# A 32-byte copy on eight rows ahead of the first store of a streaming batch norm

## The chip, the cores and the metric

The kernel runs on one core of a Trainium2 chip. The metric is the time on the device in microseconds (us) of one execution; lower is better. The core has five engines that run side by side: TensorE (not used here), VectorE (DVE in the profile), ScalarE (ACT), GpSimd (POOL) and SyncE (SP). Data moves between the memory of the chip (DRAM) and the working memory of the core (SBUF, 128 partitions) through 16 DMA engines. A DMA is issued by SyncE, ScalarE or GpSimd; each issuer has a queue of its own on every one of the 16 DMA engines (q1 for SyncE, q10 for ScalarE, q0 for GpSimd in the profile), and a semaphore that counts to 16 says that all engines have finished their share.

## The reference

Batch normalisation with given mean and variance over an array x of 32 x 256 x 128 x 128 numbers in float32 (536.87 MB), with one factor and one offset for each of the 256 channels:

```python
eps = 1e-5
mean = running_mean.reshape(1, -1, 1, 1)
var = running_var.reshape(1, -1, 1, 1)
gamma = gamma.reshape(1, -1, 1, 1)
beta = beta.reshape(1, -1, 1, 1)
return gamma * (x - mean) / np.sqrt(var + eps) + beta
```

Everything is read once and written once, so 1073.7 MB cross the DMA engines.

## The kernel before

The array is cut into 64 tiles of 128 channels by 16384 numbers: 8.39 MB each, 64 KB in each of 128 partitions, one tile for each image and half of the channels. Three buffers in SBUF (NBUF = 3) hold tiles in turn; tile i lies in buffer i mod 3. An unused tile named pad, 936 numbers wide, lies ahead of them.

At the start SyncE issues the left half of tile 0, the four parameter vectors, the right half of tile 0, and tiles 1 and 2 (lines 89 to 98). VectorE turns the parameters so that a channel lies in each partition (par), and with one square root on ScalarE makes scale_t and shift_t for each channel. Then every tile is multiplied by its scale and increased by its shift in place.

ScalarE does this for whole tiles, one instruction each (line 142). Two tiles are shared: of tile 0 VectorE does the first 6784 columns (VHEAD) and ScalarE the other 9600; of the last tile VectorE does the first 9216 (VLAST) (line 131).

When ScalarE is through with a tile, the semaphore adone goes up by one, and the tile is stored. The stores of the first 61 tiles are issued by GpSimd, the last three by ScalarE (NTAIL = 3), all on line 173. The store of tile 0 also waits for VectorE's part through vdone. When a store from buffer s has landed, which the semaphore stored[s] counts, SyncE issues the load of the tile that comes into this buffer next (line 161). So the order is a ring: load, ScalarE, store, next load, with three tiles in it at any time. No scheduler decides the order; each engine's list of instructions is as it is written, and the DMA queues are served in the order of issue.

At the end GpSimd waits for its stores and drains, and SyncE waits for all stores (lines 177 to 185).

Of the kernel before, what the change touches and what calls it, by code (L numbers as in the profile page):

```python
# [9 lines left out]
PAD = 936  # L10
NHEAD = 3
NTAIL = 3
VHEAD = 6784
VLAST = 9216


@with_exitstack
def kernel(
    ctx: ExitStack,
    tc: tile.TileContext,  # L20
    x: bass.AP,
    gamma: bass.AP,
    beta: bass.AP,
    running_mean: bass.AP,
    running_var: bass.AP,
    out: bass.AP,
):
    nc = tc.nc
    eps = 1e-5
    f32 = mybir.dt.float32  # L30

    N, C, H, W = x.shape
    P = nc.NUM_PARTITIONS
    assert C % P == 0
    NCB = C // P
    HW = H * W
    NT = N * NCB
    B = 32
    NQ = P // B
    NE = 16  # L40
    NPAR = 4

    xr = x.rearrange("n (cb p) h w -> (n cb) p (h w)", p=P)
    outr = out.rearrange("n (cb p) h w -> (n cb) p (h w)", p=P)

    params = ctx.enter_context(tc.tile_pool(name="params", bufs=1))
    data = ctx.enter_context(tc.tile_pool(name="data", bufs=1))
    params.tile([P, PAD], f32, name="pad", tag="pad")
    bufs = [data.tile([P, HW], f32, name=f"t{s}", tag=f"t{s}") for s in range(NBUF)]
    rows = params.tile([B, NPAR * C], f32, name="rows", tag="rows")  # L50
    turned = params.tile([B, NPAR * C], f32, name="turned", tag="turned")
    par = params.tile([P, NPAR, NCB], f32, name="par", tag="par")
    eps_t = params.tile([P, 1], f32, name="eps_t", tag="eps")
    std_t = params.tile([P, NCB], f32, name="std_t", tag="std")
    rstd_t = params.tile([P, NCB], f32, name="rstd_t", tag="rstd")
    scale_t = params.tile([P, NCB], f32, name="scale_t", tag="scale")
    ms_t = params.tile([P, NCB], f32, name="ms_t", tag="ms")
    shift_t = params.tile([P, NCB], f32, name="shift_t", tag="shift")

    loaded = [tc.alloc_semaphore(f"loaded{s}") for s in range(NBUF)]
    stored = [tc.alloc_semaphore(f"stored{s}") for s in range(NBUF)]
    closed = [tc.alloc_semaphore(f"closed{s}") for s in range(NBUF)]
    early = tc.alloc_semaphore("early")
    first = [tc.alloc_semaphore(f"first{s}") for s in range(NHEAD)]
    vdone = tc.alloc_semaphore("vdone")
    adone = tc.alloc_semaphore("adone")
    fetched = tc.alloc_semaphore("fetched")
    vec = tc.alloc_semaphore("vec")  # L70
    act = tc.alloc_semaphore("act")

    with tc.tile_critical():  # L73
        count = [0]

        def step(inst, sem=None, value=None):
            if sem is not None:
                inst._wait_ge(sem, value)
            elif count[0]:
                inst._wait_ge(vec, count[0])  # L80
            inst.then_inc(vec, 1)
            count[0] += 1
            return count[0]

        left, right = slice(0, HW // 2), slice(HW // 2, HW)
        last = NT - 1


        nc.sync.dma_start(out=bufs[0][:, left], in_=xr[0][:, left]).then_inc(early, 16)
        zeroed = step(nc.vector.memset(rows[:], 0.0))  # L90
        for r, ap in enumerate((running_var, gamma, beta, running_mean)):
            inst = nc.sync.dma_start(out=rows[0:NE, r * C : (r + 1) * C], in_=ap.partition_broadcast(NE))  # L92
            if r == 0:
                inst._wait_ge(vec, zeroed)
            inst.then_inc(fetched, 16)
        nc.sync.dma_start(out=bufs[0][:, right], in_=xr[0][:, right]).then_inc(first[0], 16)  # L96
        for i in range(1, NHEAD):
            nc.sync.dma_start(out=bufs[i][:], in_=xr[i]).then_inc(first[i], 16)

        def landed(i):  # L100
            if i < NHEAD:
                return first[i], 16
            s = i % NBUF
            before = 1 if s < NHEAD else 0
            return loaded[s], 16 * (i // NBUF + 1 - before)


        step(nc.vector.memset(eps_t[:], eps))  # L108
        step(nc.vector.transpose(out=turned[:], in_=rows[:]), fetched, 16 * NPAR)  # L109
        blocks = turned.rearrange("p (rc q b) -> p rc q b", q=NQ, b=B)  # L110
        flat = par.rearrange("p r cb -> p (r cb)")
        for q in range(NQ):
            placed = step(nc.vector.tensor_copy(out=flat[q * B : (q + 1) * B], in_=blocks[:, :, q, 0]))  # L113
        var_t, gamma_t, beta_t, mean_t = (par[:, r] for r in range(NPAR))
        nc.scalar.activation(  # L115
            out=std_t[:],
            in_=var_t,
            func=mybir.ActivationFunctionType.Sqrt,
            bias=eps_t[:],
            scale=1.0,  # L120
        )._wait_ge(vec, placed).then_inc(act, 1)
        step(nc.vector.reciprocal(out=rstd_t[:], in_=std_t[:]), act, 1)  # L122
        step(nc.vector.tensor_mul(out=scale_t[:], in0=gamma_t, in1=rstd_t[:]))  # L123
        step(nc.vector.tensor_mul(out=ms_t[:], in0=mean_t, in1=scale_t[:]))  # L124
        ready = step(nc.vector.tensor_sub(out=shift_t[:], in0=beta_t, in1=ms_t[:]))  # L125
        nc.vector.wait_ge(vec, ready)
        nc.scalar.wait_ge(vec, ready)

        def vector_part(i, first_col, end):
            t, cb = bufs[i % NBUF], i % NCB  # L130
            return nc.vector.tensor_scalar(  # L131
                out=t[:, first_col:end],
                in0=t[:, first_col:end],
                scalar1=scale_t[:, cb : cb + 1],
                scalar2=shift_t[:, cb : cb + 1],
                op0=mybir.AluOpType.mult,
                op1=mybir.AluOpType.add,
            ).then_inc(vdone, 1)

        def scalar_part(i, first_col):  # L140
            t, cb = bufs[i % NBUF], i % NCB
            return nc.scalar.activation(  # L142
                out=t[:, first_col:],
                in_=t[:, first_col:],
                func=mybir.ActivationFunctionType.Identity,
                bias=shift_t[:, cb : cb + 1],
                scale=scale_t[:, cb : cb + 1],
            ).then_inc(adone, 1)


        def share(i):
            return VHEAD if i == 0 else VLAST if i == last else 0

        vector_part(0, 0, VHEAD)._wait_ge(early, 16)
        nc.scalar.wait_ge(early, 16)
        vector_part(last, 0, VLAST)._wait_ge(*landed(last))


        for i in range(NHEAD, NT):
            s = i % NBUF  # L160
            inst = nc.sync.dma_start(out=bufs[s][:], in_=xr[i])
            if i >= NBUF:
                inst._wait_ge(stored[s], 16 * (i // NBUF))
            inst.then_inc(loaded[s], 16)

        for i in range(NT):
            eng = nc.gpsimd if i < NT - NTAIL else nc.scalar
            packet = {"single_packet": True} if i < NT - NTAIL else {}
            written = (stored if i < NT - NTAIL else closed)[i % NBUF]
            scalar_part(i, share(i))._wait_ge(*landed(i))  # L170
            if i in (0, last):
                eng.wait_ge(vdone, 1 if i == 0 else 2)
            eng.dma_start(out=outr[i], in_=bufs[i % NBUF][:], **packet)._wait_ge(adone, i + 1).then_inc(  # L173
                written, 16
            )


        for s in range(NBUF):
            nc.gpsimd.wait_ge(stored[s], 16 * ((NT - NTAIL - s + NBUF - 1) // NBUF))
        nc.gpsimd.drain()  # L180

        for s in range(NBUF):
            nc.sync.wait_ge(stored[s], 16 * ((NT - NTAIL - s + NBUF - 1) // NBUF))
            nc.sync.wait_ge(closed[s], 16)
# [30 lines left out]
```

## Time and profile before

| what | value |
|---|---|
| median of 3 runs | 2501.97 us (2497.04 to 2505.49) |
| the profiled execution's own time | 2502.17 us |
| its span, first to last instruction | 2500.4 us |
| ScalarE busy | 886.8 us |
| VectorE busy | 12.4 us |
| GpSimd busy | 32.7 us |
| moved by the DMA engines | 1073.84 MB, 429 GB/s over the span |
| a whole tile on ScalarE | 14.04 us |
| a load, issue to landing, median | 53.5 us |
| a store from GpSimd, issue to landing, median | 48.8 us |

The profile is of one execution, so sums are made against its own 2502.17 us, 0.20 us over the median; 1.8 us of it lie outside the span. Busy times of the engines are shares of the span. "DMA" rows give the mean busy share of the 16 DMA engines in tenths, one digit for each of 40 equal slices, and "GB/s" what they moved in each. The trace also holds a record of every DMA packet with its queue, start, length and size; a number said to be from the packet records is counted there. A row of the chain of waits has its start in us, its length in us, and what it was; a row of the timeline has the same, then the instruction, and in brackets how long the engine had been idle and what ended that.

### The profile page before, as it was taken

How to read it: one execution, taken by the hardware profiler on the slowest of the kernel's cores; microseconds unless marked ns; L12 is line 12 of the kernel's file. 1: busy time of each engine (PE TensorE's matmuls, PEld its weight loads, DVE VectorE, ACT ScalarE, POOL GpSimd, SP SyncE). 2: the span in 40 equal slices, each digit the busy share in tenths (PEclk: the TensorE clock that was granted, in tenths of full speed). 3: DMA queues.
4: the chain of work that ended last, by engine and by line, in shares of the span. 5: the costliest groups of instructions: out<-in, count | busy, mean ns of one | idle time of the engine just before them, and what ended most of it. 6: DMA issues, size and time to landing. Idle time of an engine off the chain costs nothing.

```text
span 2500.4 us, 276 instructions
## 1 busy us (share of the span) xinstructions
DVE 12.4 (0%) x13; ACT 886.8 (35%) x66; POOL 32.7 (1%) x65
## 2 busy tenths in 40 slices
DVE  1000000000000000000000000000000000000000
ACT  3243342433424234243342433424334243342422
POOL 0000000000000000000000000000000000000000
DMA  9999999999999999999999999999999999999997
GB/s 420 436 428 429 432 436 436 435 434 436 435 428 429 433 435 436 435 436 433 434 426 432 435 434 436 425 433 436 434 436 432 423 423 433 423 433 431 428 435 336
DMA packets 18707, 1073.84 MB, mean 429 GB/s; under 512 B 2128, under 2 KB 2192, under 8 KB 2192
## 3 DMA queue, kind: packets, MB, share of 16 engines
q1 hardware_dynamic: 9488, 536.94, 49.8%
q0 software_dynamic: 8784, 511.71, 47.5%
q10 hardware_dynamic: 432, 25.17, 2.3%
q14 instruction: 3, 0.02, 0.0%
HBM read 536.94 MB, written 536.87 MB: 429 GB/s over the span
## 4 chain that ended last, share of the span: by engine, by line
another core or an unknown queue 62%; ACT 35%; DMA 2%; issue 0%; SPq 0%; DVE 0%; ACTq 0%; DVEq 0%
ACT t L142 35%; DMA t<-in_x_dram 2%; SPq L92 0%; DVE rows L90 0%; ACTq L173 0%; SPq L96 0%; DVE eps_t L108 0%; DVEq L210 0%; SPq L73 0%
## 5 line engine op out<-in xcount | busy, mean ns | idle before, releaser
L142 ACT ACTIVATE t<-t,shift_t,scale_t 128x16384 f32<-128x16384 f32 (+1 forms) x64 | 885.2, 13831 | 1574.1 <-DMA t<-in_x_dram 1574.1
L173 POOL DMA_DIRECT2D out_dram<-t x61 | 32.5, 534 | 2332.7 <-ACT t L142 2332.7
L131 DVE TENSOR_SCALAR t<-t,scale_t,shift_t 128x6784 f32<-128x6784 f32 (+1 forms) x2 | 8.9, 4446 | 2448.3 <-DMA t<-in_x_dram 2448.2
L115 ACT ACTIVATE std_t<-par,eps_t 128x2 f32<-128x2 f32 x1 | 0.3, 295 | 14.3 <-DVE par L113 14.3
L115 ACT ACT_TABLE_LOAD x1 | 1.3, 1283 | 0.9 <-SPq L73 0.9
L109 DVE STREAM_TRANSPOSE turned<-rows 32x1024 f32<-32x1024 f32 x1 | 1.2, 1233 | 12.2 <-DMA rows<-in_running_mean_dram 12.2
L90 DVE MEMSET rows<- 32x1024 f32 x1 | 0.9, 912 | 1.2 <-SPq L73 1.2
L113 DVE COPY par<-turned 32x8 f32<-32x8 f32 x4 | 0.6, 162 | 0.1
L122 DVE RECIPROCAL rstd_t<-std_t 128x2 f32<-128x2 f32 x1 | 0.2, 165 | 0.4 <-ACT std_t L115 0.4
L124 DVE TENSOR_TENSOR ms_t<-par,scale_t 128x2 f32<-128x2 f32 x1 | 0.2, 161 | 0.0
L125 DVE TENSOR_TENSOR shift_t<-par,ms_t 128x2 f32<-128x2 f32 x1 | 0.2, 161 | 0.0
L123 DVE TENSOR_TENSOR scale_t<-par,rstd_t 128x2 f32<-128x2 f32 x1 | 0.2, 160 | 0.0
L199 POOL MEMSET const-bfloat16-1.0<- 128x1 bf16 x1 | 0.1, 102 | 0.0
L199 POOL MEMSET const-float32-0.0<- 128x1 f32 x1 | 0.1, 98 | 0.2 <-issue 0.2
L199 POOL MEMSET const-float32-1.0<- 128x1 f32 x1 | 0.1, 98 | 0.0
L199 POOL MEMSET const-uint8-127<- 128x1 uint8 x1 | 0.1, 98 | 0.0
L108 DVE MEMSET eps_t<- 128x1 f32 x1 | 0.1, 59 | 0.1
## 6 DMA issues: line engine op xcount, KB each, us to landing
t<-in_x_dram SPq DMA_DIRECT2D x2, 4096.0 KB, 16.1
t<-in_x_dram SPq DMA_DIRECT2D x63, 53.5
out_dram<-t POOLq DMA_DIRECT2D x61, 48.8
out_dram<-t ACTq DMA_DIRECT2D x3, 31.8
rows<-in_running_var_dram SPq DMA_DIRECT2D x1, 16.0 KB, 11.3
rows<-in_gamma_dram SPq DMA_DIRECT2D x1, 16.0 KB, 11.1
rows<-in_beta_dram SPq DMA_DIRECT2D x1, 16.0 KB, 10.9
rows<-in_running_mean_dram SPq DMA_DIRECT2D x1, 16.0 KB, 10.9
```

The costliest lines, as they stand in the source:

```text
L90: zeroed = step(nc.vector.memset(rows[:], 0.0))
L109: step(nc.vector.transpose(out=turned[:], in_=rows[:]), fetched, 16 * NPAR)
L113: placed = step(nc.vector.tensor_copy(out=flat[q * B : (q + 1) * B], in_=blocks[:, :, q, 0]))
L115: nc.scalar.activation(out=std_t[:], in_=var_t, func=mybir.ActivationFunctionType.Sqrt, bias=eps_t[:], scale=1.0,)._wait_ge(vec, placed).t ...
L122: step(nc.vector.reciprocal(out=rstd_t[:], in_=std_t[:]), act, 1)
L123: step(nc.vector.tensor_mul(out=scale_t[:], in0=gamma_t, in1=rstd_t[:]))
L124: step(nc.vector.tensor_mul(out=ms_t[:], in0=mean_t, in1=scale_t[:]))
L125: ready = step(nc.vector.tensor_sub(out=shift_t[:], in0=beta_t, in1=ms_t[:]))
L131: return nc.vector.tensor_scalar(out=t[:, first_col:end], in0=t[:, first_col:end], scalar1=scale_t[:, cb : cb + 1], scalar2=shift_t[:, cb ...
L142: return nc.scalar.activation(out=t[:, first_col:], in_=t[:, first_col:], func=mybir.ActivationFunctionType.Identity, bias=shift_t[:, cb : ...
L173: eng.dma_start(out=outr[i], in_=bufs[i % NBUF][:], **packet)._wait_ge(adone, i + 1).then_inc(written, 16)
L199: nc = _bacc.Bacc("TRN2", target_bir_lowering=False, num_devices=1)
```

## The change

GpSimd issues one more DMA, before its first store: it copies eight rows of 8 numbers (32 bytes each) from the finished parameters par to the unused tile pad, both in SBUF. The copy waits for ScalarE's part of tile 0, as the first store does, and its completion adds 16 to a new semaphore, aside. Nothing reads the copy. GpSimd waits for aside before its drain at the end, and SyncE waits for it before its last waits for the stores. Nothing else is changed.

```diff
+HALF = 8
...
-    params.tile([P, PAD], f32, name="pad", tag="pad")
+    pad = params.tile([P, PAD], f32, name="pad", tag="pad")
...
+    aside = tc.alloc_semaphore("aside")
...
             if i in (0, last):
                 eng.wait_ge(vdone, 1 if i == 0 else 2)
+            if i == 0:
+                eng.dma_start(out=pad[0:HALF, 0 : NPAR * NCB], in_=flat[0:HALF])._wait_ge(adone, 1).then_inc(aside, 16)
             eng.dma_start(out=outr[i], in_=bufs[i % NBUF][:], **packet)._wait_ge(adone, i + 1).then_inc(
                 written, 16
             )
...
+        nc.gpsimd.wait_ge(aside, 16)
         nc.gpsimd.drain()
 
+        nc.sync.wait_ge(aside, 16)
         for s in range(NBUF):
             nc.sync.wait_ge(stored[s], 16 * ((NT - NTAIL - s + NBUF - 1) // NBUF))
```

`flat` is par with its four parameters and two channel halves as 8 numbers in a row.

## The prediction

> **What bounds the kernel now.** I read the busy shares first, then the DMA queues, then the chain of waits, then short windows of the DMA traffic, and last the packet records of the trace (start, length and size of each DMA packet).
>
> The page's busy lines and DMA lines:
>
> ```profile
> DVE 12.4 (0%) x13; ACT 886.8 (35%) x66; POOL 32.7 (1%) x65
> ...
> DMA  9999999999999999999999999999999999999997
> GB/s 420 436 428 429 432 436 436 435 434 436 435 428 429 433 435 436 435 436 433 434 426 432 435 434 436 425 433 436 434 436 432 423 423 433 423 433 431 428 435 336
> ...
> q1 hardware_dynamic: 9488, 536.94, 49.8%
> q0 software_dynamic: 8784, 511.71, 47.5%
> ```
>
> No compute engine is busy more than 35% of the span; the 16 DMA engines are busy everywhere but in the last slice. Loads (q1, from SyncE) and stores (q0, from GpSimd) share them evenly.
>
> The chain of waits repeats one piece of ACT and one wait for a landing, once per tile; five of its ACT pieces:
>
> ```profile
> 89.18 14.04 ACT t L142
> ...
> 205.25 14.04 ACT t L142
> ...
> 1493.84 14.04 ACT t L142
> ...
> 1919.94 14.04 ACT t L142
> ...
> 2389.77 14.05 ACT t L142
> ```
>
> The distance between pieces is the period of a tile. Between these five lie 3, 33, 11 and 12 periods: 38.69, 39.05, 38.74 and 39.15 us, 38.99 on the mean. A period moves one load and one store, 16.78 MB; per engine that is 16 packets of 65,536 bytes. The packet records give 2.418 us for nearly every such packet, whatever the queue, and starts 2.414 us apart: 16 of them are 38.63 us. So the first stretch runs at the pace of a DMA engine, and later ones lose up to 0.5 us a period.
>
> Where that loss sits is seen in two windows of the DMA view, the first of 36 us in slices of 0.9 us, the second of 40 us in slices of 1 us, each packet counted where it starts:
>
> ```profile
> GB/s 73 0 1165 0 510 655 0 1019 146 0 1165 0 291 874 0 947 218 0 1165 0 218 947 0 801 364 0 1165 0 73 1092 0 655 510 0 1165 0 73 1092 0 583
> ...
> GB/s 66 918 66 983 66 328 721 0 983 66 524 524 0 983 66 852 197 197 786 66 983 66 524 459 66 983 66 590 393 66 983 66 983 66 262 721 66 983 66 590
> ```
>
> In the first (38 to 74 us), 1165 GB/s in 0.9 us is 16 packets: all engines start together, and queues change after each packet. In the second (1000 to 1040 us) lone 66s are single packets: an engine has fallen out of step. The landings of each transfer, counted per engine, tell the rest: until 205 us all 16 arrive within 0.7 us; then three engines fall behind the other thirteen, by 2.5 us at 284 us, 12 at 1000 us and 21 from 1500 us on. The lagging ones have no idle time from their first packet at 2.0 us to their last at 2498.25 us. Their 1024 packets at 2.414 us are 2472.3 us; the other 24 us are stretched packets, above all the first packet of a load (2.5 to 3.7 us instead of 2.418). The kernel's end is these three engines' work, and the 24 us are all that can be won.
>
> **The change, part by part.**
>
> *The copy's issue on GpSimd.* It stands after the wait for VectorE's part and itself waits for ScalarE's, so it goes where the first store goes now, and the store behind it. The timeline's rows of this place:
>
> ```profile
> 23.51 8.39 ACT L142 ACTIVATE t<-t,shift_t,scale_t 128x9600 f32<-128x9600 f32 x1 [6.74 <-DMA t<-in_x_dram]
> 32.21 0.67 POOL L173 DMA_DIRECT2D out_dram<-t  x1 [31.76 <-ACT t L142]
> ...
> 50.48 14.04 ACT L142 ACTIVATE t<-t,shift_t,scale_t 128x16384 f32<-128x16384 f32 x1 [18.59 <-DMA t<-in_x_dram]
> 64.83 0.53 POOL L173 DMA_DIRECT2D out_dram<-t  x1 [31.96 <-ACT t L142]
> 74.63 0.33 SPq L161 DMA_DIRECT2D t<-in_x_dram  x1
> ```
>
> An issue takes 0.53 to 0.67 us, so the first store is issued 0.5 to 0.7 us later. The engines have two loads queued until about 60 us, so the delay is covered: a load packet goes where a store packet would have gone. Without that cover it would cost 0.7 us, or a whole turn of 2.4 us where a slot is missed; I take 0. In the packet records the first store packet starts at 37.49 us, 5.3 us after its issue.
>
> The Trainium skill, DMA: Bandwidth & Descriptors, section "Anatomy of one DMA — SWDGE (gpsimd) path", charges a GpSimd DMA about 2.0 us whatever its size. By that rule, with nothing beside it, the sum would be 2504; the trace's engines are busy through that time, so I keep 0, and 2 us would be inside the same verdict.
>
> *The copy's packets.* 8 packets of 32 bytes and 16 completion packets of 4 bytes. The records hold 4-byte packets of 9 ns and 1,024-byte packets of 46 ns: at most 0.06 us on an engine, 0.1 as the upper end.
>
> *The turns.* The queues alternate packet by packet, and a 4-byte packet is seen to take a turn of its own queue. So the copy costs the store one turn (completion) on eight engines and two (row and completion) on the eight that carry rows. A store turn lost is a load turn won: the store ends one turn (2.41 us) later and the loads end one earlier. Now a load lands 14.5 us, six turns, after the store before it (SyncE issues on the store's landing at 74.63, the load before lands at 89.16). After the change that is four turns (9.7 us) on one half and two (4.8 us) on the other, and the halves are a turn apart: one reads while the other writes. The next load, issued at the store's landing, needs about 1.0 us to its first packet (0.96 to 1.98 us at the start), so it comes in time even with two turns, by 3.8 us. Were a third turn lost, the load queue would be empty for a moment and the engine would serve stores. A store waits in front of its queue longer than now. No engine stands idle: 0 us.
>
> *The end.* The lost turns stay lost to the last tile, since no slot is free in between. At the end the lagging engines have four packets of the last but one store left when the last load lands at 2469.27 us, 9.66 us; the last store's first packet can come 2477.0, 7.7 us after. With loads ahead of stores more is left, so that cover grows. ±1 us.
>
> *The two added waits* (GpSimd before its drain, SyncE before its last waits) are for a copy that is over before 50 us. Behind them stand only waits for the last stores. 0 to 0.1 us.
>
> *The stretched packets.* This is the one open term, 24 us now. Nothing in the trace of before shows two halves a turn apart. Lower end: all periods at the 38.63 us of the packet lengths alone, 60 x (38.99 - 38.63) = 22 us less. Upper end: periods as in the worst short stretch, 205.25 to 284.34 us, 39.55 us: 60 x 0.56 = 34 us more. I take no difference: the three engines lost the same 0.4 us a period while their distance to the others grew through every relation of reading and writing, from 2 to 21 us, so the relation between engines does not set the loss; which engine it is does.
>
> Sum: 2502.17 (this execution; span 2500.4, 1.8 around it) + 0 + 0.1 + 0 = 2502.3; the execution is 0.2 over the median of the runs, so 2502.
>
> **The rivals.**
>
> *The stretching shrinks: faster.* With halves out of step, the three engines may not be caught in the bad spot at the first packet of a load, since that would come some 5 to 12 us after the load's issue, where it now comes 16.4 us after it (74.63 to 90.99 in the packet records). For it: between 1493.84 and 1919.94 us the period is 38.74, so the loss can nearly vanish for eleven tiles. Against it: that was with the three behind as well. Price: all periods at 38.74, 60 x 0.25 = 15 us, 2487; half of it 2494.
>
> *The stretching spreads: slower.* Now eight engines, not three, come last at each load's landing, and the stretched packets sit on those that come last. Where the three were in step with each other (1919.94 to 2389.77 us, 39.15 us) their first load packets took 2.6 to 3.7 us at the same time. With eight in step from the start the whole run could go like that or worse: 60 x 0.16 = 10 us, 2512; at twice that excess 2522. It decides from a mean period of 39.12 us on.
>
> *The copy takes no turns* (its packets come while the load packet before is still running, 34.55 to 37.5 us): then all stays in step and the time is that of before, within the forecast.
>
> *The lag is a property of the engines.* The Trainium skill, DMA: Bandwidth & Descriptors, section "Latency and other measured facts", says that DMA engines 7 and 15 are usually slower in traces and guesses at contention on the ports of GpSimd's descriptor rings. The trace agrees that a few fixed engines lag (three, by 21 us), and by that rule a copy at the start changes nothing.
>
> **How the numbers follow.** Forecast, no difference beyond 0.3% (7.5 us, about what a measurement of this kernel can tell from no change; the runs of before span 8.5 us), with the copy that takes no turns in it: 0.40. Stretching shrinks by more than a third of its 24 us: 0.29. Stretching spreads: 0.31, a little more, since its price has no ceiling while the gain is bounded by 24 us. The range runs from 2484 (nearly all won) to 2518 (a third to a half of the upper end). The time of the likeliest case alone would be 2495 to 2509.
>
> **What would show it.** Right: the copy's row and the first store 0.5 to 0.7 us apart on GpSimd; a window of 38 to 74 us in which no slice holds 16 packet starts but two groups of eight alternate; the first load of SyncE's loop issued 2.4 to 5 us later than 74.63, the third tile landed 2 to 5 us before 89.16; mean period 38.9 to 39.1 us. Wrong: the mean period below 38.87 (faster) or above 39.12 (slower), engines idle in the middle of the run, or a tail in which the last store waits.

## The result, and the profile after

The changed kernel takes 2487.78 us in the median of 22 runs (2485.61 to 2500.54); the kernel before, in 22 runs beside them, 2500.7 us (2483.61 to 2514.36). The ratio is 0.9959, 95% interval 0.9944 to 0.9975: faster by 0.4%. The profiled execution took 2490.27 us with a span of 2488.5 us, 11.9 us less than the one of before.

Busy time, DMA and issue lines of the page of the changed kernel:

```profile
span 2488.5 us, 278 instructions
...
DVE 12.4 (0%) x13; ACT 886.8 (36%) x66; POOL 33.4 (1%) x66
...
GB/s 420 423 438 437 436 423 436 438 438 423 436 438 437 429 432 436 437 434 428 436 436 436 429 431 438 433 429 436 437 436 429 434 437 437 430 432 437 436 431 358
...
t<-in_x_dram SPq DMA_DIRECT2D x63, 44.0
out_dram<-t POOLq DMA_DIRECT2D x61, 58.0
...
pad<-par POOLq DMA_DIRECT2D x1, 0.2 KB, 8.2
```

The engines do what they did before. New is the last group: a load now lands 44.0 us after its issue (53.5 before), a store 58.0 us after its issue (48.8 before). The sum of the two is about the same, 102.0 against 102.3 us. The copy lands 8.2 us after its issue.

The timeline around the first store of the changed kernel (start, length, instruction, idle time before it):

```profile
23.38 8.39 ACT L144 ACTIVATE t<-t,shift_t,scale_t 128x9600 f32<-128x9600 f32 x1 [6.87 <-DMA t<-in_x_dram]
32.07 0.66 POOL L176 DMA_DIRECT2D pad<-par  x1 [31.62 <-ACT t L144]
32.72 0.57 POOL L177 DMA_DIRECT2D out_dram<-t  x1
45.76 14.04 ACT L144 ACTIVATE t<-t,shift_t,scale_t 128x16384 f32<-128x16384 f32 x1 [13.99 <-DMA t<-in_x_dram]
...
79.59 39.03 SPq L163 DMA_DIRECT2D t<-in_x_dram  x2
84.48 14.04 ACT L144 ACTIVATE t<-t,shift_t,scale_t 128x16384 f32<-128x16384 f32 x1 [24.68 <-DMA t<-in_x_dram]
```

The store is issued 0.65 us after the copy. Tile 1 is there at 45.7 us (50.5 before), tile 2 at 84.45 us (89.16 before), and SyncE issues its first load of the loop, on the landing of the first store, at 79.59 us (74.63 before). So the stores moved back by 5.0 us and the loads forward by 4.7 us: two turns of 2.41 us each. The next load now lies issued for 4.9 us before the load ahead of it has landed, not for 14.5 us.

The DMA traffic from 38 to 74 us, in slices of 0.9 us, shows that this holds for all 16 engines:

```profile
GB/s 0 874 291 0 291 874 0 874 291 0 1165 0 73 1092 0 874 291 0 1165 0 0 1165 0 728 437 0 1165 0 0 1165 0 510 655 0 1019 146 0 1165 0 364
```

1165 GB/s is again 16 packets that start in one slice. There are no two groups of eight. The packet records say why: at 36.8 to 37.3 us eight engines have a 32-byte packet of the copy, and at 37.1 to 37.5 us the other eight have a 4-byte packet instead; at 39.2 to 40.0 us all 16 have a 4-byte completion. Every engine has lost two store turns.

Where the time went, by the landings of the loads: tile 2 lands 4.7 us earlier; the 58 periods from there to tile 60 take 38.81 us on the mean in place of 38.995, 10.7 us in all; from the landing of tile 60 to the last store it is 151.2 us in place of 147.8, 3.4 us more. 4.7 + 10.7 - 3.4 = 12.0 us. What the shift gives at the start is mostly paid back at the end; the gain is in the periods. In the changed kernel one engine lags instead of three. In the landings of the stores it comes 12 us behind its nearest neighbour from about 1500 us on, and almost all of that is lost before 1330 us. In the landings of the loads the 16 engines stay within 4.4 us of each other up to tile 61, where the kernel before had 21 us between the first and the last. The windows view, before and then after, from 1900 to 2400 us (stretch, length, busy times, clock, DMA share, GB/s):

```profile
1900.00:2400.00 500.00, 0.00 (x0) 178.70 (x13) 6.37 (x12) 1.00 1.00 429
```

```profile
1900.00:2400.00 500.00, 0.00 (x0) 182.51 (x13) 6.40 (x12) 1.00 1.00 434
```

The DMA engines are busy all the time in both; in the changed kernel they move 434 GB/s, which is what they moved from 74 to 230 us in either.

### The profile page after: what moved, and what is told of

It is laid out like the page before. It is cut to its first block, busy times and chain, and to the rows that moved or that the text cites. A ratio compares the mean times of both kernels' runs of the same rounds, so it can differ in the third digit from the quotient of the medians.

```text
span 2488.5 us, 278 instructions
## 1 busy us (share of the span) xinstructions
DVE 12.4 (0%) x13; ACT 886.8 (36%) x66; POOL 33.4 (1%) x66
## 4 chain that ended last, share of the span: by engine, by line
another core or an unknown queue 93%; DMA 4%; SPq 1%; ACT 1%; issue 0%; DVE 0%; POOL 0%; DVEq 0%
DMA t<-in_x_dram 2%; DMA out_dram<-t 2%; SPq L163 1%; ACT t L144 1%; SPq L94 0%; DVE rows L92 0%; POOL pad L176 0%; DVE eps_t L110 0%; DVEq L216 0%; SPq L75 0%
## 5 line engine op out<-in xcount | busy, mean ns | idle before, releaser
L111 DVE STREAM_TRANSPOSE turned<-rows 32x1024 f32<-32x1024 f32 x1 | 1.2, 1232 | 11.9 <-DMA rows<-in_running_mean_dram 11.9
## 6 DMA issues: line engine op xcount, KB each, us to landing
rows<-in_running_mean_dram SPq DMA_DIRECT2D x1, 16.0 KB, 10.7
```

## The experiments

Three theories stood at first. Theory 1: what helps is the shift by two turns. Theory 2: the copy itself helps, by moving the descriptor ring on or by warming GpSimd's way of issuing a DMA. The third, the split into halves, was the forecast's and is tried on its own below. "Turns" is the distance from a store's landing to the next load's landing, in turns of 2.41 us; "lying time" is how long a load lies issued until the load ahead of it has landed on the last engine; the median of the load's issue-to-landing time less one period (38.7 us) gives it within 0.4 us. "Stretch" is the time by which the first packets of loads exceed 2.418 us in one execution, summed over the engines, counting packets over 2.44 us.

| kernel | turns | lying time, us | mean period from tile 2 to 60, us | stretch, us | median, us | ratio to before, 95% |
|---|---|---|---|---|---|---|
| before | 6 | 14.5 | 38.995 | 49 | 2500.7 | 1 |
| after | 2 | 5.1 | 38.81 | 6 | 2487.78 | 0.9959 (0.9944 to 0.9975) |
| e_early | 6 | 14.5 | 39.00 | 37 | 2506.77 | 1.0025 (1.0005 to 1.0045) |
| e_late2 | 2 | 5.1 | 38.725 | 12 | 2490.05 | 0.9971 (0.994 to 1.0003) |
| e_undo | 6 | 14.5 | 39.07 | 67 | 2506.08 | 1.0018 (0.9998 to 1.0038) |
| e_phi10 | 7 to 8 | 19.3 | 38.96 | 92 | 2510.93 | 1.0027 (0.9996 to 1.0058) |
| e_late1 | 4 | 9.7 | 39.125 | 49 | 2511.67 | 1.0029 (1.0008 to 1.0049) |
| e_delay | 8 | 6.1 | 38.81 | 11 | 2491.56 | 0.995 (0.993 to 0.997) |
| e_half | 6 and 2 | 13.4 | 38.76 | 40 | 2491.04 | 0.9966 (0.9933 to 0.9998) |
| e_mid | 6, then 2 | 14.5, then 5.1 | 38.79 | 33 | 2500.66 | 0.9984 (0.9956 to 1.0011) |
| e_delay8 | 6 | 5.7 | 38.76 | 12 | 2489.78 | 0.9945 (0.9923 to 0.9966) |
| e_delay4 | 6 | 10.1 | 39.06 | 31 | 2507.28 | 0.9991 (0.9969 to 1.0013) |
| e_late1_delay4 | 4 | 5.2 | 38.93 | 22 | 2495.33 | 0.9946 (0.9925 to 0.9967) |
| e_late2_delay2 | 4 | 7.4 | 38.96 | 31 | 2501.43 | 0.9974 (0.9949 to 1.0) |

Times and ratios are of 9 to 22 runs; the four columns before them are of one profiled execution each, so a row's period need not stand for its median. Single runs scatter: of the 22 of the kernel before, three lie below 2488 us, and of the 22 of the changed kernel two lie above 2500 us. None of these five was profiled. The kernels of the first four experiments (to e_phi10), of the next four and of the last four were run together; the kernel before had medians of 2503.5, 2504.9 and 2504.6 us beside them, and each ratio is to the runs beside it.

### The copy without the lost turns: e_early

```diff
+        nc.gpsimd.dma_start(out=pad[0:HALF, 0 : NPAR * NCB], in_=flat[0:HALF])._wait_ge(vec, placed).then_inc(aside, 16)
         var_t, gamma_t, beta_t, mean_t = (par[:, r] for r in range(NPAR))
...
-            if i == 0:
-                eng.dma_start(out=pad[0:HALF, 0 : NPAR * NCB], in_=flat[0:HALF])._wait_ge(adone, 1).then_inc(aside, 16)
```

> The copy is issued at about 16 us, as soon as the parameters are in place, long before the first store; its packets then take no turn from a store. Theory 1 (turns: what helps is that the store stream starts two turns later, so that a load lands 2 turns after a store and not 6): the distance from a store's landing to the next load's landing is again 14.5 us, and the time is that of the kernel before, ratio 0.998 to 1.002. Theory 2 (the copy itself: the descriptor ring moved on, or GpSimd's DMA path warmed): ratio 0.994 to 0.998 as in the changed kernel.

The copy's and the loads' issue lines:

```profile
t<-in_x_dram SPq DMA_DIRECT2D x63, 53.5
...
pad<-par POOLq DMA_DIRECT2D x1, 0.2 KB, 6.9
```

The copy is there, the loads land after 53.5 us as before the change, and the gain is gone: 1.0025 (1.0005 to 1.0045). That speaks against theory 2.

### The lost turns without the copy: e_late2

```diff
-VHEAD = 6784
+VHEAD = 1152
```

> No copy. VectorE has 1152 columns of tile 0 in place of 6784, so ScalarE's part takes about 4.8 us longer and the first store is issued at about 37.0 us in place of 32.2, two turns later. Theory 1: distance store landing to load landing 4.8 us (2 turns), SyncE's first loop load issued at about 79.5 us, ratio 0.994 to 0.998. Theory 2: no copy, so ratio 1.000 to 1.003.

```profile
t<-in_x_dram SPq DMA_DIRECT2D x63, 43.8
out_dram<-t POOLq DMA_DIRECT2D x61, 57.9
```

SyncE's first loop load is issued at 79.25 us, and the issue lines above are those of the changed kernel. The median is 2490.05 us, the ratio 0.9971 with an interval that just reaches 1.0003: eight of the twelve runs lie between 2484 and 2495 us, four between 2500 and 2519. Theory 1 has the better of it, but the two-turn state alone does not make every run fast.

### Taking the turns back: e_undo and e_phi10

Both add one DMA on SyncE, the first to the changed kernel, the second to the kernel before (with pad named as in the change). At the end SyncE waits for it, too:

```diff
+            if i == 2:
+                nc.sync.dma_start(out=pad[0:16, 16:24], in_=gamma[0:8].partition_broadcast(16)).then_inc(slot, 16)
             nc.sync.dma_start(out=bufs[i][:], in_=xr[i]).then_inc(first[i], 16)
```

> The changed kernel, and SyncE puts a DMA of 16 rows of 32 bytes between the loads of tiles 1 and 2, whose row and completion packets take two turns from the loads on each engine. Theory 1: the distance goes back to 6 turns (14.5 us) with the copy still in place, ratio 0.998 to 1.002. Theory 2: ratio 0.994 to 0.998.

> The kernel before, with only that DMA of 16 rows between the loads of tiles 1 and 2: the loads lose two turns. Theory 1: distance 10 turns (24 us); if the loss grows with the distance, ratio 1.002 to 1.008. Theory 2: ratio 0.999 to 1.001.

The issue line of the loads in e_undo:

```profile
t<-in_x_dram SPq DMA_DIRECT2D x63, 53.5
```

With the copy in place but the loads two turns back, the kernel is as slow as before, 1.0018 (0.9998 to 1.0038): theory 1 again. In e_phi10 the first loads came out at 10 turns as meant (24.2 us), but the store queue then ran empty and the distance settled between 17 and 19.5 us; the loads lie issued for 19.3 us, the stretch of their first packets is the largest of all, 92 us, and the median 2510.93 us. The interval does not exclude 1.

### Is it the distance, or how early the load is issued? e_late1 and e_delay

If only the distance counted, four turns should lie between six and two.

```diff
-VHEAD = 6784
+VHEAD = 3968
```

> No copy; VectorE has 3968 columns of tile 0 in place of 6784, so the first store is issued about 2.4 us later, one turn. Distance from a store's landing to the next load's landing 9.7 us (4 turns). If the loss grows with this distance: between the 6-turn and the 2-turn kernels, ratio 0.996 to 1.000; if only two turns help, 0.999 to 1.002.

It does not. The issue line of the loads:

```profile
t<-in_x_dram SPq DMA_DIRECT2D x63, 48.8
```

The loads lie issued for 9.7 us, and the kernel is slower than the one before, 1.0029 (1.0008 to 1.0049). The loss does not fall evenly with the distance.

The second kernel leaves the first store alone and holds back the loads. VectorE, which is idle in the loop, writes zeros to pad NPAUSE times after each store's landing, and SyncE waits for that; VectorE's part of the last tile comes after the loop.

```diff
+NPAUSE = 12
...
-                inst._wait_ge(stored[s], 16 * (i // NBUF))
+                nc.vector.wait_ge(stored[s], 16 * (i // NBUF))
+                for k in range(NPAUSE):
+                    paused += 1
+                    nc.vector.memset(pad[:], 0.0).then_inc(later, 1)
+                    nc.vector.wait_ge(later, paused)
+                inst._wait_ge(later, paused)
```

> The kernel before, with the first store where it was, but SyncE's loop loads wait for 12 small memsets that VectorE does after the store has landed, about 10 us. The distance on the slowest engine stays 14.5 us (6 turns); only the load is issued later, some 4.5 us before the slowest engine needs it, so the other engines cannot read ahead of it by more than that. Theory 1a (what counts is beside which store packet a load begins, so the distance): time as before, ratio 0.999 to 1.002, first packets of loads stretched as before (37 to 67 us in sum over the engines). Theory 1b (what counts is how long a load lies issued before the slowest engine begins it, so how far the others run ahead): ratio 0.994 to 0.998, with the stretch of first packets near the 6 to 12 us of the 2-turn kernels.

The lines of the loop and of its issues:

```profile
L168 DVE MEMSET pad<- 128x936 f32 x732 | 613.4, 838 | 1781.0 <-DMA out_dram<-t 1605.2 <-DVE pad L168 175.8
```

```profile
t<-in_x_dram SPq DMA_DIRECT2D x63, 44.7
out_dram<-t POOLq DMA_DIRECT2D x61, 43.6
```

A memset took 0.84 us and the wait between two 0.26 us, so the pause was 13.2 us and not the 10 that were meant. The load queue ran dry once a period and the distance went to 19.4 us, 8 turns. Yet all twelve runs lie between 2488 and 2496 us, ratio 0.995 (0.993 to 0.997), and the stretch is 11 us. A larger distance with a short lying time is fast, which points to the lying time. The other half of what was expected failed: the other engines still ran up to 17 us ahead of the last one before the last two loads, so it is not that they are held close.

### Doses of the pause: e_delay8, e_delay4, e_late1_delay4, e_late2_delay2

The same kernel with NPAUSE 8 and 4; and with NPAUSE 4 and VHEAD 3968, NPAUSE 2 and VHEAD 1152.

> 8 memsets in place of 12, so SyncE's loop loads are issued 8.8 us after the store's landing and lie issued 5.7 us before the slowest engine needs them; the load queue does not run empty and the distance stays 14.5 us (6 turns). If the time a load lies issued is what sets the loss: ratio 0.993 to 0.997, mean period of tiles 11 to 60 38.6 to 38.75. If the 12 memsets helped because the load queue ran empty (distance 19.4 us in that run): ratio 0.999 to 1.002.

> 4 memsets: loads issued 4.4 us after the landing, lying issued about 10 us, as in the 4-turn kernel; distance 14.5 us. If the lying time sets the loss with a limit between 5.7 and 9.7 us: ratio 0.999 to 1.003. If any pause on VectorE helps: 0.994 to 0.998.

> The 4-turn kernel (3968 columns on VectorE, no copy), which lost 0.3%, with 4 memsets: loads lie issued 5.3 us in place of 9.7. If the lying time sets the loss: ratio 0.993 to 0.997. If the distance of 4 turns is bad for itself: 1.001 to 1.005.

> The 2-turn kernel without a copy (1152 columns on VectorE) with 2 memsets: loads lie issued about 2.7 us in place of 4.9, still in time for the slowest engine. If a shorter lying time helps further: ratio 0.992 to 0.996, without the runs above 2500 us that the 2-turn kernel had. If 5 us is already enough: 0.994 to 0.998, the same as at 2 turns.

The timeline of e_delay8 around its first loop load:

```profile
75.61 0.84 DVE L168 MEMSET pad<- 128x936 f32 x1 [54.18 <-DMA out_dram<-t]
...
83.31 0.84 DVE L168 MEMSET pad<- 128x936 f32 x1 [0.26 <-DVE pad L168]
84.18 40.47 SPq L163 DMA_DIRECT2D t<-in_x_dram  x2
91.37 14.04 ACT L144 ACTIVATE t<-t,shift_t,scale_t 128x16384 f32<-128x16384 f32 x1 [26.41 <-DMA t<-in_x_dram]
```

The issue lines of e_delay8, then of e_delay4:

```profile
t<-in_x_dram SPq DMA_DIRECT2D x63, 44.3
out_dram<-t POOLq DMA_DIRECT2D x61, 48.4
```

```profile
t<-in_x_dram SPq DMA_DIRECT2D x63, 49.2
out_dram<-t POOLq DMA_DIRECT2D x61, 48.9
```

Both have the six turns of the kernel before and its store times (48.4 and 48.9 against 48.8 us). They differ in the loads alone: lying for 5.7 us the kernel is fast, 0.9945 (0.9923 to 0.9966), with periods of 38.64 us from tile 21 on; lying for 10.1 us it is as before, 0.9991 (0.9969 to 1.0013). This is the cleanest pair; the two also differ in the four more memsets of a pause, but the changed kernel is fast without any. With four turns, the same pause turns the slow e_late1 into 0.9946 (0.9925 to 0.9967). In e_late2_delay2 the pause made the load come too late for the slowest engine; the queue ran dry, the distance went to four turns (9.7 us) and the lying time to 7.4 us, not the 2.7 us that were meant; at 0.9974 (0.9949 to 1.0) it stands between. It says nothing on shorter lying times.

### The split into halves, and the copy in the middle: e_half and e_mid

e_half is e_undo with 8 rows in place of 16 in SyncE's DMA; in e_mid the copy stands ahead of store 20 and waits for the same part of ScalarE as that store:

```diff
-            if i == 0:
+            if i == 20:
```

> The changed kernel, and between the loads of tiles 1 and 2 SyncE puts a DMA of 8 rows, which should take two load turns on eight of the engines and none on the others: eight engines at 6 turns, eight at 2, which is the split that the prediction expected of the change. If the split itself helps: ratio under 0.996. If each engine's distance counts for itself: the lagging engines are among those at 6 turns, ratio 0.998 to 1.002.

> The copy is issued ahead of store 20 in place of store 0, at about 820 us: 6 turns before that, 2 after. Theory 1 (turns): mean period 38.95 to 39.1 us up to there and 38.6 to 38.8 behind it, ratio 0.995 to 0.999. If only the state of the first tiles counts: periods as in the kernel before throughout, ratio 0.999 to 1.002.

The issue line of the loads in e_half:

```profile
t<-in_x_dram SPq DMA_DIRECT2D x63, 52.0
```

An engine with two turns and the last ones at 12 to 13 us of distance are both seen in the packet records, so the split is there. The ratio is 0.9966 (0.9933 to 0.9998), with runs from 2486 to 2511 us. It lies between the two expectations, and its interval reaches into both. From tile 21 to 51 the period is 38.64 us and the engines' distances to each other stand still, though the loads lie issued for 13.4 us for the last engines.

The packet records show how far this goes against the lying time. In the kernel before, of the first packets of loads that began less than 11 us after the load's issue, 9 of 592 took over 2.44 us, 2 us too long in all; of those that began later, 109 of 335, 47 us too long. In e_half 42 of the 456 late ones did, 20 us too long. So a long wait is where the stretch sits in the kernel before, but a long wait alone does not bring it: the split may help in a way of its own. That stays open.

In e_mid the periods are 39.2 us over tiles 3 to 11 and 38.76 us over tiles 21 to 61, with 39.02 us between them once the two turns that the loads gain at tile 20 are added back. That is the direction that theory 1 asks for; the ratio, 0.9984 (0.9956 to 1.0011), lies within the 0.995 to 0.999 that it gives, but the interval does not exclude 1.

No version here beats the changed kernel clearly: e_delay8 and e_late1_delay4 have ratios like its own, with medians of 2489.78 and 2495.33 us.

## Why the prediction was right or wrong

*The bound* was read rightly. The time is that of the DMA engines that lag, and the gain lies in stretched packets: the periods shortened by 0.19 us each while ScalarE's and VectorE's busy times stayed at 886.8 and 12.4 us.

*The issue* (0.5 to 0.7 us, covered) came out at 0.65 us, and the engines went on with load packets.

*The turns* were half right. That tiny packets take whole turns, that a lost store turn is a load turn won, and what that does to the landings all came as worked out: 79.59 us and 84.45 us lie in the ranges given. But not "one turn on eight engines and two on the eight that carry rows": the engines without rows had a 4-byte packet in the rows' place, so all lost two, and the copy put no engine out of step with another. The Trainium skill, DMA: Bandwidth & Descriptors, section "Why a DMA increments its semaphore by 16 and not by 1", says that on GpSimd's path all 16 engines post the completion whatever the shape; the trace agrees, with 16 completions, but holds the eight 4-byte packets besides.

*The end* was put at ±1 us. From the landing of tile 60 to the last store it takes 3.4 us more, but that is the other side of the shift, which had brought the loads 4.7 us forward; start and end together give 1.3 us. The last engine to finish has no gap before its last packet, as worked out.

*The copy's cost* as a GpSimd DMA was kept at 0 against the 2.0 us that the Trainium skill, DMA: Bandwidth & Descriptors, section "Anatomy of one DMA — SWDGE (gpsimd) path", charges. The copy landed after 8.2 us, since it waited its turns beside 64 KB packets of the loads, and the engines moved those meanwhile.

*The step that failed is the stretched packets*, put at "no difference" because "the relation between engines does not set the loss; which engine it is does". In the runs the loss is not fixed: the excess of the loads' first packets went from 49 to 6 us, and the mean period from 38.995 to 38.81 us, below the 38.87 us that was named as a sign of being wrong. What moved it is how long a load lies issued before the slowest engine begins it: with the same six turns and the same store times, 5.7 us gave 0.9945 (e_delay8) and 10.1 us 0.9991 (e_delay4). Among the kernels only e_half, at 13.4 us and 0.9966, does not fit, and single runs scatter to both sides. How a long wait stretches a packet stays open.

The rival "the stretching shrinks" named this very thing, the time from a load's issue to its first packet, beside a wrong reason (halves out of step), and its price was near: periods of 38.74 us and 2487 us, where 38.81 us and, in the median, 2487.78 us were measured. That the two times are this close is in part luck, since the profiled execution, with its periods of 38.81 us, took 2490.27 us and the shift itself gave 1.3 us that the price did not hold. The range of 2484 to 2518 us holds the measured time because it was drawn over the rivals; the likeliest case alone, 2495 to 2509 us, does not. The evidence for this rival stood in the trace: the stretch sat on first packets of loads, and the change moved exactly their issue. The argument used against it, that the loss was the same at every distance between lagging and other engines, held the lying time at 14.5 us throughout and so could not speak of it. Nor was the loss the same: the prediction's own stretch from 1493.84 to 1919.94 us, with periods of 38.74 us, lost 0.1 us a period and not 0.4.

The other rule named, in the Trainium skill, DMA: Bandwidth & Descriptors, section "Latency and other measured facts" (engines 7 and 15 usually slower), was read as no change. The trace carries no engine numbers, so whether these are the lagging ones is not seen; that a later issue of the loads takes away half or more of what the periods lose over 38.63 us is (38.995 us before, 38.81 us in the changed kernel, 38.76 us in e_delay8).

## What to carry to other kernels

In this kernel, where loads and stores fill the DMA engines and take turns packet by packet, a DMA of 256 bytes cost its queue two whole turns, and this shifted the two streams against each other for the rest of the run. In a kernel of this kind, look at the issue-to-landing times of both streams, not at the bytes. Issuing a load earlier was not free here: but for e_half, loads that lay issued for 10 to 19 us cost about half a per cent against loads that lay for 5 to 6 us. When all engines of a resource look busy, look at how long single packets take and whether a few engines fall behind.

## What the runs showed of the hardware that was not expected

A load's first packet took up to 4.1 us in place of 2.418 us (e_undo; 3.8 us in the kernel before). In the executions in which loads lay issued for about 10 us or more, this stretch came to 31 to 92 us in sum over the engines; in those with 5 to 6 us, to 6 to 22 us. Why it meets only some of the 16 engines, and whether the time counts or the number of packets still ahead in the queue (about one at 5 us, two at 10 us, three at 14.5 us), no run here tells.

Stores are stretched too, but elsewhere: in the kernel before 106 of their packets took over 2.44 us, up to 3.9 us, 95 us too long in all. Nearly all of them came after 1470 us and sat on engines that ran ahead, almost none on the three that lag. In the changed kernel it was 6 packets and 0.5 us.

Between tiles 3 and 11 every kernel lost 0.2 to 1.0 us a period over 38.63 us, whatever the lying time; from tile 21 on most of the short-lying ones run at 38.64 to 38.73 us (e_late1_delay4 at 38.92 us). What ends that is open too.

A copy of eight rows from GpSimd put a packet on all 16 engines, twice: eight of 32 bytes and eight of 4 bytes at 36.8 to 37.5 us, then 16 of 4 bytes.
